# A hybrid encoder layer on one core: stores and small loads become steps of their own in the planner, VectorE and GpSimd are kept apart in its plan, and matmuls that depend on other engines are planned later

## The chip, the cores and the metric

The kernel runs on one core of one Trainium2 chip. A core has five engines with a queue of instructions each: TensorE (PE, with its weight loads shown apart as PEld), VectorE (DVE), ScalarE (ACT), GpSimd (POOL) and SyncE (SP), which here issues every DMA. Each engine works through its own queue in the order in which the program was written; semaphores hold an instruction until what it needs is there. The metric is the device time of one execution in microseconds.

## What is computed

One step of a one-layer streaming encoder, for 1024 frames of a new stream (the prompt) and 32 frames of a running one (the sample), in one array of 1056 frames. Cut to what matters:

```python
h = rmsnorm(x, g_mix_norm);  z = h @ w_in            # 1024 -> 8192
qa, ka, va, qr, kr, vr, g_ret, gate_a, gate_r = split(z)
qa, ka = rmsnorm(qa), rmsnorm(ka)                    # per head, 2 x 64
# 8 heads of differential attention, chunk-causal; sample: with a cache of 512 keys
s = einsum(qa, ka) * 64**-0.5;  p = softmax(s)       # two maps per head
o_a = rmsnorm((p[0] - lam * p[1]) @ va) * g_sub
# 8 heads of retention with decay, from a running state
o_r = rmsnorm((rotary(qr) @ rotary(kr).T * d_mat) @ vr + q @ S * q_decay) * silu(g_ret)
x = x + (sigmoid(gate_a) * o_a + sigmoid(gate_r) * o_r) @ w_o
x = x + (silu(h2 @ w_ff_gate) * (h2 @ w_ff_up)) @ w_ff_down      # h2 = rmsnorm(x), 2816 wide
y = x + sigmoid(rmsnorm(x) @ w_ple_gate) * (p_in @ w_ple)
# outputs: y, the new keys and values (ka, va), the final retention states
```

## The kernel before

Products in float32 accuracy are made of three float16 products: each operand is split in a high and a low part (`mm3`, lines L748 to L750 for the projection, L488 to L490 elsewhere).

The program has a head stage and then a merge and feed-forward stage. **The head stage** goes through 72 units, a unit being one head h (8) and one tile of frames i (9 tiles, the last with the 32 sample frames). For each unit PE makes two projections, A (q, k, v and rotary q, k) and, four units later (`LAG`), B (retention values and gates). Each is 8 times three matmuls of 128x512 into one of three PSUM banks `pj`.

What follows an A projection is `unit_a`: ACT takes the projection out of PSUM, DVE and GpSimd normalize and scale q and k, `kv` (L1055, GpSimd) is the key to be stored; SP stores it (L1056), transposes q and k by DMA (L1080 `q`, L1082 `kT`); PE makes the scores `sc` (L889 to L892), DVE the row maximum (L899), DVE or GpSimd the bias `nb` (L901), ACT the exponentials (L909); DVE combines the two maps and splits the result (L923 to L937; the high part by ACT L933 or DVE L935), SP transposes it by DMA (`aT`, L942), PE multiplies with v (`po`, L950 to L954), and the head's output `oa` is normalized (L971). `values` makes v and, on GpSimd, the rotation (L983 to L991).

What follows a B projection is `unit_b` with `retention`: PE transposes the rotated q and k (`pr`, L1144), DVE or ACT copies the result out (`copy`, L402: `qz` and `qT`), PE multiplies (L1157 to L1160), DVE masks (`inn`, L1163), PE multiplies again (`por`, L1165); then norm, gates and the sum with `oa` (L1230), a DMA transpose (`mixT`, L1244) and a store into scratch memory (`mix_d`, L1248). At the end the eight rows of `mix_d` are read back as `mixs`, the operand of the next stage. Beside this the weights of the next head are loaded, 1 MB at a time (L421), scaled and split (L473 to L481); `cache_steps` does so for the cached keys and values.

**What sets the order.** The order of PE, DVE, ACT and GpSimd, and with it that of the DMAs on SP, is made at build time by a planner, `Flow`. Each piece of work is a generator. It yields the engine that it needs and how long the planner shall take it to be (`V` for DVE, `S` for ACT, `G` for GpSimd, `M` for PE, `DM` and `X` for the DMA path, `either` where two engines will do), and then writes its instruction; `get` and `put` take and return buffers, `wait` and `set` are events, `delay` passes time. `Flow.run` takes the piece that can start first, by its own clock, and so fixes the program's order; a DMA that is written without a yield comes where its generator happens to be, right behind its producer. A result of DVE, ACT or GpSimd is taken to be usable after `LAT` = 0.13 more, and a matmul that comes behind such a step after another `MARGIN` = 0.3. On the chip none of these times is kept: only the order is.

The second stage (output projection, gate and up products in a seven-product scheme, and the first part of the down product) has a `Flow` of its own; the rest is written in program order.

Of the kernel before, what the change touches and what calls it, by code (L numbers as in the profile page):

```python
# [21 lines left out]
P = 128  # L22
# [24 lines left out]
MARGIN = 0.3  # L47
# [10 lines left out]

def V(n, f=1.0, x=0.0):
    return {"V": 0.07 + x + f * n / 960.0}  # L60
# [6 lines left out]
def G(n, x=0.0):  # L67
    return {"G": 0.15 + x + 0.0021 * n}
# [129 lines left out]
def kernel(  # L198
# [81 lines left out]
    def spread_max(amax, n, tag, at_bank=None):  # L280


        if at_bank is None:
            yield ("wait", "id")
        key, pool = at_bank or ("o", ps_o)
        yield ("get", key)
        yield M(0.1)
        pt = pool.tile([P, 512], F32, tag=key, name="mt")
        nc.tensor.transpose(out=pt[0:n, 0:P], in_=amax, identity=id32)
        yield V(P)  # L290
# [109 lines left out]

    def copy(e, out, in_):
        (nc.scalar.copy if e == "S" else ENG[e].tensor_copy)(out, in_)  # L402
# [3 lines left out]
    def load_block_steps(src, w, b, gi, tag, rowf, out, tail=False, due=None, late=None, hold=None):  # L406
# [19 lines left out]
        for q in range(4):  # L426
# [9 lines left out]
            yield V(512)  # L436
# [65 lines left out]
    with ExitStack() as pa:  # L502
# [98 lines left out]
        def const_b():  # L601
# [44 lines left out]
            yield V(128)  # L646
# [5 lines left out]
            yield V(128)  # L652
# [29 lines left out]
        def norm_x(i):  # L682
# [34 lines left out]
            for b in range(2):  # L717
# [12 lines left out]
                g = yield either(S(4 * R), V(4 * R))  # L730
                copy(g, hi, pt)
                yield V(4 * R)
# [29 lines left out]
        def fold(i, ps):  # L762
# [8 lines left out]
            yield V(P)  # L771
# [7 lines left out]
        def rms_small(ss, R, n, tag):  # L779

            yield G(0, 0.5 + 0.2 * n)
# [5 lines left out]
        def prep_head_a(h, w, e):  # L787
# [7 lines left out]
            s0 = s02[:, h % 2]  # L795
            nc.sync.dma_start(out=s0[0:64], in_=st0[h])
            gr = hp.tile([P, P], F32, tag="grn", name="grn", bufs=2)
            nc.sync.dma_start(out=gr, in_=grn[h])
# [8 lines left out]
        def cache_steps(h, dA, e):  # L807
# [24 lines left out]
            yield V(1, 1.0, 0.3)  # L832
# [45 lines left out]
        def attend(key, i, R, q4, sblocks, masked, vblocks, NK, sc_ap, do_ap):  # L878
# [3 lines left out]
            for ms in ((0, 1),) if NK <= 512 else ((0,), (1,)):  # L882
# [13 lines left out]
                yield V(NK * len(ms))  # L896
# [96 lines left out]
        def values(h, i, R, ps, kv, zr, dA, e, buf, key):  # L993
# [14 lines left out]
            yield V(P)  # L1008
# [9 lines left out]
        def unit_a(h, i, ps, dA, e):  # L1018
# [25 lines left out]
            yield V(256)  # L1044
# [11 lines left out]
            nc.sync.dma_start(out=kvo[h, t0:t0 + RT], in_=kv[0:RT])  # L1056
            yield ("later", ("kv", 3.0))
# [44 lines left out]
        def prep_head_b(h, w, e):  # L1102
# [8 lines left out]
            yield V(128)  # L1111
# [26 lines left out]
        def retention(h, i, R, vr, e, box):  # L1138
# [7 lines left out]
            g = yield either(V(128), S(128, -0.06))  # L1146
            copy(g, q0[0:64], pr[64:128, 0:P])
            g = yield either(V(128), S(128, -0.06))
# [12 lines left out]
            yield V(128)  # L1161
# [7 lines left out]
            yield V(128)  # L1169
# [11 lines left out]
            if i >= NT - 2:  # L1181
                nc.sync.dma_start(out=ro[i - (NT - 2), h], in_=Sq)

        def unit_b(h, i, ps, dB, e):
# [18 lines left out]
            yield V(P)  # L1203
# [14 lines left out]
            yield V(P, 1.0, 0.06)  # L1218
# [28 lines left out]
            yield X(0.05)  # L1247
            nc.sync.dma_start(out=mix_d[h, :, :, t0:t0 + RT], in_=mt[:, :, 0:RT])  # L1248
            yield ("later", ("mix", 2.2))
# [50 lines left out]
        def load_ple():  # L1300
# [4 lines left out]
            for n, (src, c, o) in enumerate(((pT, T, 0), (wple, D, 4 * T))):  # L1305
# [8 lines left out]
                for q, (k, cs) in enumerate(cuts):  # L1314
                    yield V(c // 2)
                    nc.vector.tensor_reduce(out=am4[:, q:q + 1], in_=st[:, k, cs], axis=AX.X, op=ALU.max, apply_absolute_value=True)
                yield V(4)
# [18 lines left out]
        def ple(part):  # L1336
# [3 lines left out]
            for m in (2 * part,):  # L1340
                for pair in (((m, 0), (m, 1)), ((m + 1, 0), (m + 1, 1)), ((m, 2), (m + 1, 2))):
                    for n, (j, c) in enumerate(pair):
# [8 lines left out]
                        g = yield either(S(CH), V(CH))  # L1351
# [14 lines left out]
        def last_mix():  # L1366
            for i in range(NT):
                yield ("wait", ("b", H - 1, i))
            nc.sync.dma_start(out=tail["mixs"][:, H - 1], in_=mix_d[H - 1])

        def stream():
# [10 lines left out]
            for s in range(NT * H + LAG):  # L1382
# [37 lines left out]
                if s >= LAG:  # L1420
# [16 lines left out]
            for part in range(4):  # L1437
# [3 lines left out]
                         ret=2, th=2, xc=3, su=1, ms=2))  # L1441
# [22 lines left out]
    with ExitStack() as pc:  # L1464
# [18 lines left out]
        with ExitStack() as pw:  # L1483
# [73 lines left out]
            def residual(c):  # L1557
# [10 lines left out]
                for m in range(KD):  # L1568
                    yield ("wait", ("wo", c, m))
                    yield V(CW, 1.0, 0.08)  # L1570
# [24 lines left out]
                yield V(4, 1.0, 0.1)  # L1595
                v = sm(4, "nbv")
                nc.vector.tensor_scalar(out=v[0:B], in0=ps[0:B, CW:CW + 4], scalar1=_f(1.0 / D), scalar2=EPS, op0=ALU.mult, op1=ALU.add)
                yield G(4, 0.2)
# [11 lines left out]
                for k in (0, 4, 1, 5, 2, 6, 3, 7):  # L1610
                    yield V(CW, 1.0, 0.08)
# [132 lines left out]
            def gu_sums(j, p):  # L1744
# [12 lines left out]
                def comb(out, in0, ps, op=ALU.add):  # L1757
                    yield V(CW, 1.0, 0.06)
# [331 lines left out]
```

## Time and profile before

| | us |
|---|---|
| median of three runs | 1901.42 (1895.13 to 1901.45) |
| the profiled execution | 1898.33 |
| its span, first to last instruction | 1896.5 |
| PE, DVE, ACT, GpSimd busy in the span | 1808.5, 1474.4, 1063.3, 715.1 |
| first matmul of a projection, last of a projection | 17.9, 1006.9 |
| first matmul of the output projection | 1038.9 |

A few words on how the profile is read. A line such as L950 is a line of the kernel before. "Busy" of PE counts a matmul until its modelled end; matmuls overlap, so that a 128x512 matmul is shown with some 0.38 us although the next one starts 0.216 us behind it. A loss on PE is therefore read best from one start to the next. A wait row names the engine, tile and line that waited, and behind the arrow what ended the wait; SPq is SyncE's queue, where a DMA that waits holds back all that is queued behind it. "Granted clock" is TensorE's clock as a share of the full one.

### The profile page before, as it was taken

What the parts mean: (1) busy time and instruction counts of PE and PEld (TensorE: products, weight loads), DVE (VectorE), ACT (ScalarE), POOL (GpSimd) and SP (SyncE); (2) the same over time, 40 slices, a digit from 0 to 9 for tenths busy, and PEclk for the clock granted to TensorE, in tenths of its full rate; (3) what the DMA queues carried; (4) which work ended last, traced back from release to release, by engine and by line L of the source; (5) the groups of instructions that cost most, each with busy time, mean ns of one, the idle gap of its engine ahead of it and who ended that gap; (6) DMA issues with size and microseconds to landing.
All of it is one profiled execution on the core that took longest, in us unless ns stands there. A gap on an engine that the chain in (4) does not pass through costs nothing.

```text
span 1896.5 us, 37208 instructions
## 1 busy us (share of the span) xinstructions
PE 1808.5 (95%) x13391; PEld 1152.9 (61%) x13391; DVE 1474.4 (78%) x3784; ACT 1063.3 (56%) x2762; POOL 715.1 (38%) x1161
## 2 busy tenths in 40 slices
PE   6889999999999989999998998999999999999999
PEld 3455455555555545555555686777777776666666
DVE  7878887887877878878886489999999986644364
ACT  7667766676675756767665345555555542101132
POOL 3646454454654554545441167323232300000010
PEclk9999999999999999999999999999999999999999
DMA  5344433444443433443438421221212116112031
GB/s 198 101 115 108 111 83 88 110 92 117 90 99 89 101 97 79 123 99 88 110 79 265 163 65 49 80 102 68 79 45 68 45 62 256 62 62 88 2 134 50
DMA packets 234251, 186.06 MB, mean 98 GB/s; under 512 B 187569, under 2 KB 214449, under 8 KB 226130
## 3 DMA queue, kind: packets, MB, share of 16 engines
q1 hardware_dynamic: 234066, 183.69, 35.0%
q8 instruction: 105, 1.72, 0.4%
q14 instruction: 80, 0.66, 0.1%
HBM read 113.09 MB, written 31.34 MB: 76 GB/s over the span
## 4 chain that ended last, share of the span: by engine, by line
PE 58%; DVE 17%; POOL 8%; ACT 7%; DMA 5%; issue 4%; SPq 0%; POOLq 0%; DVEq 0%; ACTq 0%
PE ps L488 9%; PE ps L490 9%; PE ps L489 9%; PE ps L1479 4%; PE pj L748 4%; PE pj L749 4%; PE ps L1478 4%; PE pj L750 4%; PE ps L1477 4%; DMA aT<-p 3%; ACT p L909 2%; DVE nm L899 2%; POOL qkr L784 2%; DVE w L481 1%; DVE w L1630 1%
## 5 line engine op out<-in xcount | busy, mean ns | idle before, releaser
L748 PE MATMUL pj<-w,xh 128*128 128x512 f16 x1024 | 390.8, 382 | 2.8 <-ACT w L479 2.8
L749 PE MATMUL pj<-w,xh 128*128 128x512 f16 x1024 | 390.6, 381 | 0.6 <-DVE w L481 0.6
L750 PE MATMUL pj<-w,xh 128*128 128x512 f16 x1024 | 390.4, 381 | 0.0
L489 PE MATMUL ps<-mixs,w 128*128 128x352 f16 (+1 forms) x960 | 262.5, 279 | 5.9 <-DVE mixs L1502 5.9
L488 PE MATMUL ps<-mixs,w 128*128 128x352 f16 (+1 forms) x960 | 262.4, 278 | 0.3 <-DVE o1c L244 0.3
L490 PE MATMUL ps<-mixs,w 128*128 128x352 f16 (+1 forms) x960 | 262.4, 278 | 0.0
L490 PEld LDWEIGHTS <-w 128*128 128x128 f16 x1736 | 170.9, 98 | 57.3 <-issue 6.0
L488 PEld LDWEIGHTS <-w 128*128 128x128 f16 x1736 | 171.1, 99 | 56.2 <-issue 4.8
L489 PEld LDWEIGHTS <-w 128*128 128x128 f16 x1736 | 170.8, 98 | 53.0 <-issue 3.6
L1635 POOL TENSOR_TENSOR st<-st 128x512 f32<-128x512 f32 x66 | 88.5, 1341 | 244.7 <-DVE w L1630 186.7
L750 PEld LDWEIGHTS <-xh 128*128 128x128 f16 x1024 | 100.5, 98 | 123.5 <-issue 3.8
L748 PEld LDWEIGHTS <-xh 128*128 128x128 f16 x1024 | 101.0, 99 | 91.6 <-issue 6.5
L909 ACT ACTIVATE p<-sc,nb,scs 128x896 f32<-128x896 f32 (+7 forms) x128 | 106.3, 831 | 87.6 <-POOL nb L901 52.5
L749 PEld LDWEIGHTS <-xh 128*128 128x128 f16 x1024 | 100.5, 98 | 87.3 <-issue 4.3
L488 PE MATMUL ps<-tT,w 128*128 128x352 f16 (+1 forms) x528 | 143.7, 277 | 0.0
L489 PE MATMUL ps<-tT,w 128*128 128x352 f16 (+1 forms) x528 | 143.6, 277 | 0.0
L490 PE MATMUL ps<-tT,w 128*128 128x352 f16 (+1 forms) x528 | 143.6, 277 | 0.0
L1630 DVE SCALAR_TENSOR_TENSOR w<-st,gus,w 128x512 f16<-128x512 f32 x132 | 140.6, 1066 | 0.1
L899 DVE TENSOR_REDUCE nm<-sc 128x1 f32<-128x640 f32 (+6 forms) x112 | 102.7, 917 | 26.1 <-PE sc L892 25.6
L1479 PE MATMUL ps<-a,w 128*128 128x352 f16 x312 | 97.5, 313 | 0.5 <-DVE w L1721 0.5
L1477 PE MATMUL ps<-a,w 128*128 128x352 f16 x312 | 97.5, 313 | 0.0
L1478 PE MATMUL ps<-a,w 128*128 128x352 f16 x312 | 97.5, 313 | 0.0
(422 smaller groups left out, 4650.4 us busy)
## 6 DMA issues: line engine op xcount, KB each, us to landing
st<-in_win_dram SPq DMA_DIRECT2D x30, 1024.0 KB, 5.3
st<-in_wgu_dram SPq DMA_DIRECT2D x22, 1024.0 KB, 4.8
st<-in_wdn_dram SPq DMA_DIRECT2D x16, 704.0 KB, 5.4
out_dram<-kv SPq DMA_DIRECT2D x64, 128.0 KB, 1.9
a_d<-a SPq DMA_DIRECT2D x9, 528.0 KB, 2.6
b<-a_d SPq DMA_DIRECT2D x9, 528.0 KB, 7.5
mixs<-mix_d SPq DMA_DIRECT2D x8, 528.0 KB, 6.5
pw_d<-pws SPq DMA_DIRECT2D x12, 352.0 KB, 4.2
```

The source lines that it names most:

```text
L488: nc.tensor.matmul(out=ps, lhsT=wh, rhs=ah, start=first, stop=False)
L489: nc.tensor.matmul(out=ps, lhsT=wh, rhs=al, start=False, stop=False)
L490: nc.tensor.matmul(out=ps, lhsT=wl, rhs=ah, start=False, stop=last)
L748: nc.tensor.matmul(out=ps, lhsT=xhi, rhs=w[:, k, 0], start=(k == 0), stop=False)
L749: nc.tensor.matmul(out=ps, lhsT=xhi, rhs=w[:, k, 1], start=False, stop=False)
L750: nc.tensor.matmul(out=ps, lhsT=xh[:, k, 1, t0:t0 + P], rhs=w[:, k, 0], start=False, stop=(k == KD - 1))
L899: nc.vector.tensor_reduce(out=nm[0:R, mc], in_=pv, axis=AX.X, op=ALU.max, negate=True)
L909: nc.scalar.activation(pt[0:R, 0:NK], ps[0:R, p0:p0 + NK], AF.Exp, bias=nb[0:R, m:m + 1], scale=sc_ap[0:R], accum_out=Z[0:R, m:m + 1])
L1477: nc.tensor.matmul(out=ps, lhsT=wt[:, 0, j], rhs=a[:, 0, cs], start=(first and j == js[0]), stop=False)
L1478: nc.tensor.matmul(out=ps, lhsT=wt[:, 1, j], rhs=a[:, 0, cs], start=False, stop=False)
L1479: nc.tensor.matmul(out=ps, lhsT=wt[:, 2, j], rhs=a[:, 1, cs], start=False, stop=(last and j == js[-1]))
L1630: nc.vector.scalar_tensor_tensor(out=w[:, i, 1], in0=src, scalar=s, in1=w[:, i, 0], op0=ALU.mult, op1=ALU.subtract)
```

## The change

Four things are changed; the arithmetic and the number of instructions stay (the choice of engine for the `either` steps aside).

1. `MARGIN` goes from 0.3 to 0.8: a matmul that depends on another engine is planned 0.5 later. This holds for both planners.
2. In the head stage's planner a step of DVE that is marked as working on SBUF (`V`, now an `Own`) and one of GpSimd (`G`) may not overlap. Steps that read or write PSUM, reductions and GpSimd's small power steps are marked `VP` and `GP`, which do not take the lock. Some forty yields are renamed so; two are shown.
3. Stores (`kvo`, `ro`, `mix_d`) become generators of their own, planned 2.0, 1.0 and 1.0 behind their producer, with 0.5 of the DMA path each.
4. Small loads (retention state, norm gains, cache) get a yield of the DMA path each, and the read-back of `mix_d` as `mixs` waits for the stores row by row.

```diff
-MARGIN = 0.3
+MARGIN = 0.8
...
+class Own(float):
+    pass
+
 def V(n, f=1.0, x=0.0):
+    return {"V": Own(0.07 + x + f * n / 960.0)}
+
+def VP(n, f=1.0, x=0.0):
     return {"V": 0.07 + x + f * n / 960.0}
...
 def G(n, x=0.0):
+    return {"G": Own(0.15 + x + 0.0021 * n)}
+
+def GP(n, x=0.0):
     return {"G": 0.15 + x + 0.0021 * n}
...
 class Flow:
-    def __init__(self, buffers):
+    def __init__(self, buffers, shared=False):
+        self.shared = shared
         self.free = {e: 0.0 for e in "MVSGD"}
+        self.port = {"V": 0.0, "G": 0.0}
...
                     start = max(c[3], self.free[e])
+                    if self.shared and isinstance(us, Own):
+                        start = max(start, self.port["G" if e == "V" else "V"])
...
             self.free[e] = start + us
+            if isinstance(us, Own):
+                self.port[e] = start + us
...
+    def store(out, in_, key, us, event=None):
+        yield ("delay", us)
+        yield X(0.5)
+        nc.sync.dma_start(out=out, in_=in_)
+        if event:
+            yield ("set", event)
+        if key:
+            yield ("delay", 2.5)
+            yield ("put", key)
...
-            nc.sync.dma_start(out=kvo[h, t0:t0 + RT], in_=kv[0:RT])
-            yield ("later", ("kv", 3.0))
+            flow.add(store(kvo[h, t0:t0 + RT], kv[0:RT], "kv", 2.0))
...
-            yield X(0.05)
-            nc.sync.dma_start(out=mix_d[h, :, :, t0:t0 + RT], in_=mt[:, :, 0:RT])
-            yield ("later", ("mix", 2.2))
+            flow.add(store(mix_d[h, :, :, t0:t0 + RT], mt[:, :, 0:RT], "mix", 1.0, ("m", h, i)))
...
-            nc.sync.dma_start(out=kc[0:64], in_=ckT[h])
-            nc.sync.dma_start(out=kc[64:128], in_=ckT[h])
-            nc.sync.dma_start(out=vc, in_=cv[h])
-            yield ("delay", 6.0)
+            for dst, src in ((kc[0:64], ckT[h]), (kc[64:128], ckT[h]), (vc, cv[h])):
+                yield X(0.9)
+                nc.sync.dma_start(out=dst, in_=src)
+            yield ("delay", 4.0)
...
-            yield V(NK * len(ms))
+            yield VP(NK * len(ms))
...
-            g = yield either(V(128), S(128, -0.06))
+            g = yield either(VP(128), S(128, -0.06))
...
         def last_mix():
-            for i in range(NT):
-                yield ("wait", ("b", H - 1, i))
-            nc.sync.dma_start(out=tail["mixs"][:, H - 1], in_=mix_d[H - 1])
+            for j in range(H):
+                for i in range(NT):
+                    yield ("wait", ("m", j, i))
+                yield X(0.5)
+                nc.sync.dma_start(out=tail["mixs"][:, j], in_=mix_d[j])
...
-                        for j in range(H - 1):
-                            nc.sync.dma_start(out=tail["mixs"][:, j], in_=mix_d[j])
...
-                         ret=2, th=2, xc=3, su=1, ms=2))
+                         ret=2, th=2, xc=3, su=1, ms=2), True)
```

What this does to the order is shown at two places. Line numbers after the change are some 30 higher (L1157 becomes L1187, L942 becomes L973, both stores become L423), the names stay.

The first is PE's queue in the retention of head 2, tile 6 (`pr` and `por` are its PSUM tiles, `pj` the projection that runs meanwhile), from the transpose to the next matmul of the same unit. Before:

```order
L1144 MATMUL pr<-cst_sb,qk 128x128
L748 LDWEIGHTS xh
L748 MATMUL pj<-w,xh 128x512
...
L750 LDWEIGHTS xh
L750 MATMUL pj<-w,xh 128x512
L1157 MATMUL pr<-qz_130,qT 128x128
L1159 MATMUL por<-S_134,qz_130 128x128
```

Six matmuls of the projection stand between L1144 and L1157. After the change the same place reads:

```order
L1174 MATMUL pr<-cst_sb,qk 128x128
L777 LDWEIGHTS xh
L777 MATMUL pj<-w,xh 128x512
...
L981 MATMUL po<-vcs,aT 128x128
...
L779 LDWEIGHTS xh
L779 MATMUL pj<-w,xh 128x512
L1187 MATMUL pr<-qz_130,qT 128x128
L1189 MATMUL por<-S_134,qz_130 128x128
```

Now nine matmuls of the projection and the fifteen short ones of another unit's `po` stand there.

The second is SP's queue at the `aT` transpose of head 3, tile 3 (`st` is a 1 MB load of weights, `mix_d` a store of the B side, `mixT` its transpose). Before:

```order
L1244 DMA_TRANSPOSE mixT<-ms 128x2x32
L1080 DMA_TRANSPOSE q_6735<-qst 128x2x128
L1082 DMA_TRANSPOSE kT<-qst 128x4x128
L421 DMA st<-in_win_dram 128x2048
L942 DMA_TRANSPOSE aT<-p 128x8x128
L1248 DMA mix_d<-mixT 256x1x32
```

The load stands ahead of the transpose, the store behind it. After:

```order
L1110 DMA_TRANSPOSE q_6682<-qst 128x2x128
L1112 DMA_TRANSPOSE kT<-qst 128x4x128
L1274 DMA_TRANSPOSE mixT<-ms 128x2x32
L423 DMA mix_d<-mixT 256x1x32
L973 DMA_TRANSPOSE aT<-p 128x8x128
L450 DMA st<-in_win_dram 128x2048
```

The load has moved behind the transpose and the store of `mix_d` ahead of it.

More of the change, by code (lines that the diff above doesn't have):

```diff
@@ L289, in spread_max @@
         nc.tensor.transpose(out=pt[0:n, 0:P], in_=amax, identity=id32)
-        yield V(P)
+        yield VP(P)
         mc = sm(1, tag + "mc")
@@ L435, in load_block_steps @@
                 continue
-            yield V(512)
+            yield VP(512)
             if rowf is None:
@@ L651, in const_b @@
             ls = sm(2, "ls")
-            yield V(128)
+            yield VP(128)
             nc.vector.tensor_reduce(out=ls, in_=lam_sb[:, 0].rearrange("p (b c) -> p b c", b=2), axis=AX.X, op=ALU.add)
@@ L729, in norm_x @@
                 hi, lo = [xh[:, ks, a, i * P:i * P + P] if i < NT - 1 else xs[:, ks, a * TS:(a + 1) * TS] for a in range(2)]
-                g = yield either(S(4 * R), V(4 * R))
+                g = yield either(S(4 * R), VP(4 * R))
                 copy(g, hi, pt)
-                yield V(4 * R)
+                yield VP(4 * R)
                 nc.vector.tensor_tensor(out=lo, in0=pt, in1=hi, op=ALU.subtract)
@@ L770, in fold @@
             nc.scalar.copy(su, psv[:, :, 1])
-            yield V(P)
+            yield VP(P)
             nc.vector.tensor_tensor(out=suz[:, :, 0:TS], in0=psv[:, :, 0], in1=su, op=ALU.add)
@@ L779, in rms_small @@
         def rms_small(ss, R, n, tag):
-            yield G(0, 0.5 + 0.2 * n)
+            yield GP(0, 0.5 + 0.2 * n)
             r = sm(n, tag + "r", 6)
@@ L795, in prep_head_a @@
             s0 = s02[:, h % 2]
+            yield X(0.5)
             nc.sync.dma_start(out=s0[0:64], in_=st0[h])
             gr = hp.tile([P, P], F32, tag="grn", name="grn", bufs=2)
+            yield X(0.5)
             nc.sync.dma_start(out=gr, in_=grn[h])
@@ L831, in cache_steps @@
             ar = sm(2, "car")
-            yield V(1, 1.0, 0.3)
+            yield VP(1, 1.0, 0.3)
             nc.vector.tensor_tensor(out=ar[:, 0:1], in0=pt[:, 0:1], in1=kbound, op=ALU.max)
@@ L1007, in values @@
                                      scale=e["ddec"][0:R, b:b + 1])
-            yield V(P)
+            yield VP(P)
             nc.vector.scalar_tensor_tensor(out=vh[0:R, i, 1], in0=ps[0:R, 256:384], scalar=vs_, in1=vh[0:R, i, 0],
@@ L1043, in unit_a @@
             nc.scalar.activation(sq[0:R], zg[0:R], AF.Square, scale=0.125)
-            yield V(256)
+            yield VP(256)
             ss = sm(4, "qss", 6)
@@ L1110, in prep_head_b @@
             dB = w[1]
-            yield V(128)
+            yield VP(128)
             nc.vector.tensor_reduce(out=mbr, in_=e["gr"], axis=AX.X, op=ALU.max, apply_absolute_value=True)
@@ L1160, in retention @@
             nc.tensor.matmul(out=pr[:, 384:512], lhsT=qk[:, (h * NT + i) % NQ], rhs=vr, start=True, stop=True)
-            yield V(128)
+            yield VP(128)
             inn = wk.tile([P, P], F32, tag="inn", name="inn")
@@ L1168, in retention @@
             gT = _f((1.0 - 2.0 ** (-5 - h)) ** (P if i < NT - 1 else TS))
-            yield V(128)
+            yield VP(128)
             Sn = S2[:, (h * NT + i) % 2]
@@ L1181, in retention @@
             if i >= NT - 2:
-                nc.sync.dma_start(out=ro[i - (NT - 2), h], in_=Sq)
+                flow.add(store(ro[i - (NT - 2), h], Sq, None, 1.0))
         def unit_b(h, i, ps, dB, e):
@@ L1201, in unit_b @@
                                  scale=hdB[0:R, 1:2])
-            yield V(P)
+            yield VP(P)
             gu = wk.tile([P, P], F32, tag="gu", name="gu")
@@ L1217, in unit_b @@
             r = yield from rms_small(ss, R, 1, "or")
-            yield V(P, 1.0, 0.06)
+            yield VP(P, 1.0, 0.06)
             of = wk.tile([P, P], F32, tag="orf", name="orf", bufs=3)
@@ L1314, in load_ple @@
                 for q, (k, cs) in enumerate(cuts):
-                    yield V(c // 2)
+                    yield VP(c // 2)
                     nc.vector.tensor_reduce(out=am4[:, q:q + 1], in_=st[:, k, cs], axis=AX.X, op=ALU.max, apply_absolute_value=True)
-                yield V(4)
+                yield VP(4)
                 am = sm(1, "wam", 3)
@@ L1350, in ple @@
                             yield ("get", "p")
-                        g = yield either(S(CH), V(CH))
+                        g = yield either(S(CH), VP(CH))
                         if n == 0:
@@ L1594, in residual @@
                                          rhs=ones32[:, 0:1], start=(j == 0), stop=(j + 1 == n))
-                yield V(4, 1.0, 0.1)
+                yield VP(4, 1.0, 0.1)
                 v = sm(4, "nbv")
                 nc.vector.tensor_scalar(out=v[0:B], in0=ps[0:B, CW:CW + 4], scalar1=_f(1.0 / D), scalar2=EPS, op0=ALU.mult, op1=ALU.add)
-                yield G(4, 0.2)
+                yield GP(4, 0.2)
                 r = sm(4, "nbr")
@@ L1610, in residual @@
                 for k in (0, 4, 1, 5, 2, 6, 3, 7):
-                    yield V(CW, 1.0, 0.08)
+                    yield VP(CW, 1.0, 0.08)
                     nc.vector.scalar_tensor_tensor(out=xf[:, k], in0=xf[:, k], scalar=gS[:, 1, k:k + 1], in1=ps[:, 0:CW],
@@ L1757, in comb @@
                 def comb(out, in0, ps, op=ALU.add):
-                    yield V(CW, 1.0, 0.06)
+                    yield VP(CW, 1.0, 0.06)
                     nc.vector.tensor_tensor(out=out, in0=in0, in1=ps, op=op)
```

7 lines of the change are left out of this document (4 added, 3 removed).

## The prediction

> **What bounds the kernel now.** I read the busy time by stage first, then PE's waits in the longest stage, then the timeline at single waits, and last SP's queue. The stages (columns: window, its length, busy time of PE, PEld, DVE, ACT and GpSimd with instruction counts, granted clock, DMA share, GB/s):
>
> ```profile
> 0.00:50.00 50.00, 35.53 (x154) 18.18 (x155) 37.67 (x120) 36.84 (x79) 19.64 (x39) 1.00 0.60 200
> 50.00:1005.00 955.00, 902.99 (x6283) 505.00 (x6281) 766.42 (x2263) 655.84 (x1942) 500.01 (x957) 0.99 0.42 98
> 1005.00:1040.00 35.00, 29.37 (x208) 19.43 (x205) 22.10 (x75) 18.55 (x45) 2.96 (x7) 0.92 0.93 312
> 1040.00:1180.00 140.00, 128.88 (x1070) 95.86 (x1068) 105.99 (x200) 60.20 (x127) 69.05 (x60) 0.95 0.28 93
> 1180.00:1897.00 717.00, 711.74 (x5689) 514.47 (x5686) 542.26 (x1131) 291.88 (x573) 123.44 (x101) 1.00 0.23 81
> ```
>
> PE is busy almost throughout, so its work is the floor and only its waits can be won: 5 us behind 1180, where nothing is to be had, and 955 - 903 = 52 us in the head stage, which is the part that the change reorders. Who ends them there (total, times, longest):
>
> ```profile
> PE po L950 <- DMA aT<-p: 23.9, 16, 4.5
> PE pr L1157 <- DVE qT L402: 5.1, 9, 1.0
> PE sc L889 <- ACT p L909: 5.1, 8, 1.3
> PE pr L1157 <- ACT qT L402: 4.3, 7, 1.1
> PE t L722 <- DVE w L712: 3.5, 2, 1.9
> PE sc L889 <- DMA kT<-qst: 3.1, 3, 1.3
> PE por L1165 <- DVE inn L1163: 3.1, 6, 0.9
> PE mt L314 <- DVE wamh L447: 2.3, 4, 0.7
> ```
>
> These 50 us are nearly all of it, and no projection (L748) is among them: PE never waits for a `pj` bank. But idle time hides a part, as one place shows (start, duration):
>
> ```profile
> 405.28 0.28 PE L1144 MATMUL pr<-cst_sb,qk 128*128 128x128 f32 x1
> 405.39 0.38 PE L748 MATMUL pj<-w,xh 128*128 128x512 f16 x1
> ...
> 406.26 0.38 PE L749 MATMUL pj<-w,xh 128*128 128x512 f16 x1
> 406.47 0.38 PE L750 MATMUL pj<-w,xh 128*128 128x512 f16 x1
> 406.94 0.49 PE L1157 MATMUL pr<-qz,qT 128*128 128x128 f32 x2
> ```
>
> A matmul of 512 columns takes 0.216 from start to start; L1157 starts 0.47 behind L750, so 0.25 us is lost although no gap is shown. Counted so, start to start against the usual spacing of each form over the 6283 matmuls of the window, the loss is 71 us: some 27 at L950, 14 at L1157, 12 at L889, 7 at L1165, 4 at L722, 3 at L314, 4 elsewhere. That is the purse. A part of the clock comes on top (below).
>
> **The change part by part.** *MARGIN.* Six projection matmuls, 1.3 us, stand between L1144 and L1157 at this place, and the chain through two copies took 0.25 longer. Over all 72 units the order before has 1.8 us of PE work there, the order after 2.6; between L1160 and L1165 it is 1.6 and 2.0 (row counts of the two orders, each row at the spacing of its form in the trace). The same 0.8 taken off each of the 72 losses at L1157 leaves 2 of 14; 0.4 at L1165 leaves 2.5 of 7. **Minus 12 and minus 4.5.** The work that fills the gap is the projection that has to be done anyway. What is late next is the rest of the unit, the norm and the gates, whose result is first wanted after the unit's own `oa`, and that is early.
>
> *Scores.* L889 waits for the one `sc` bank, until ACT's exponentials end, and for `kT`. The 0.5 of MARGIN taken off its losses leaves 5 of 12, but transposes of q now stand right behind a 1 MB load 14 times where it was 7. What such a neighbour does, from issue to landing for L1080 (min, median, max) and in one wait at `aT`:
>
> ```profile
> DMA to landing us min/median/max: 2.3/2.8/6.3
> ...
> 448.69 0.53 SPq L421 DMA_DIRECT2D st<-in_win_dram  x1
> 449.32 1.24 SPq L942 DMA_TRANSPOSE aT<-p  x1
> ...
> 455.40 0.23 PE L950 MATMUL po<-vh,aT 128*128 128x128 f16 x1 [0.74 <-DMA aT<-p]
> ```
>
> At the worst 7 x 3.5 = 24 us come back; at the best nothing, since the distance from the end of an A projection to its scores grows from 16 to 20 us of PE work. I take 3 back, near the lower end, because 3.8 us of new distance exceeds the 3.5: **minus 4** for L889 with that.
>
> *The `aT` transposes, stores and loads.* Two causes show. One is the load just seen: the transpose took 6 us to land. In the order after, `aT` stands right behind a load 5 times, not 15. The other is a store that waits on SP:
>
> ```profile
> 530.79 0.36 SPq L421 DMA_DIRECT2D st<-in_win_dram  x1
> 538.87 0.33 SPq L1056 DMA_DIRECT2D out_dram<-kv  x1
> 539.31 1.20 SPq L942 DMA_TRANSPOSE aT<-p  x1
> ...
> 536.25 0.48 DVE L937 SCALAR_TENSOR_TENSOR p<-p,lsc 128x256 f16<-128x256 f32 x1
> ...
> 541.78 0.23 PE L950 MATMUL po<-vh,aT 128*128 128x128 f16 x1 [1.06 <-DMA aT<-p]
> ...
> SPq L1056 <- POOL kv L1055: 118.2, 42, 8.9
> SPq L1248 <- DMA mixT<-ms: 55.3, 42, 3.8
> ```
>
> The data of the transpose were ready at 536.7; SP stood at the store of `kv` until 538.9, and PE lost 1.2 us. The last two rows are all such waits of the stores in the stage. In the plan a store now comes 1 to 2 us later, so more of what is ready passes it. Against this, `aT` stands right behind a store of `mix_d` 40 times, not 22, and a store waits 55.3 / 42 = 1.3 us for its transpose. From the scores to `po` there is 0.8 us more PE work than before (13.0 against 12.2), but half of that was there already as lost time. Bounds: all 27 go, or, with 18 x 1.3 = 23 us of new SP waits and no cover, as good as none do. I take 12 left, **minus 15**: by their neighbours in SP's rows, 13 of the 19 large losses have one of the two causes right ahead of them.
>
> *The lock in the plan.* 65 instructions leave GpSimd for DVE, and 16 splits go from DVE to ACT (count, min/median/max ns):
>
> ```profile
> L901 POOL TENSOR_SCALAR nb<-nm,scs x68: 282/358/1576, 54.7 to 982.8; 128x1 f32<-128x1 f32 x44, 128x2 f32<-128x2 f32 x24
> L901 DVE TENSOR_SCALAR nb<-nm,scs x28: 195/208/279, 89.7 to 973.4; 128x1 f32<-128x1 f32 x20, 128x2 f32<-128x2 f32 x8
> L1052 DVE TENSOR_TENSOR z<-z,gqk x49: 407/424/673, 38.2 to 974.1; 128x256 f32<-128x256 f32 x49
> L1234 DVE TENSOR_TENSOR mx<-mx,orf x44: 270/292/559, 85.9 to 1013.4; 128x128 f32<-128x128 f32 x44
> L1234 POOL TENSOR_TENSOR mx<-mx,orf x28: 447/456/1482, 107.1 to 1023.0; 128x128 f32<-128x128 f32 x28
> L935 DVE TENSOR_SCALAR p<-p,lsc x30: 273/542/1039, 60.9 to 995.5; 128x640 f16<-128x640 f32 x9, 128x384 f16<-128x384 f32 x5, 128x896 f16<-128x896 f32 x5, 128x512 f16<-128x512 f32 x4
> L933 ACT ACTIVATE p<-p,lsc x42: 388/828/1148, 67.4 to 986.7; 128x256 f16<-128x256 f32 x8, 128x640 f16<-128x640 f32 x7, 128x768 f16<-128x768 f32 x7, 128x1024 f16<-128x1024 f32 x5
> ```
>
> DVE gets 32 `nb` at 0.208, 19 operations on `z` at 0.424, 14 of 128x128 and 5 copies at 0.292: 20 us, less 16 splits at 0.542, 9: plus 12 us on 766. ACT gets the 16 at 0.828, 13 us; GpSimd loses over 20. All three have 200 to 450 us of idle time in the stage, so this costs PE nothing by itself; were DVE's cover gone, 12 us. Medians of the DVE rows lie 4 to 8% above their minima, so that keeping the two engines apart can give DVE 0.04 x 766 = 30 us at most, beside PE's work; I take 0 (as a rival: below).
>
> *Clock.* Two waits and the windows of 50 us around them:
>
> ```profile
> 302.07 0.29 PE L950 MATMUL po<-vh,aT 128*128 128x128 f16 x1 [2.33 <-DMA aT<-p]
> ...
> 300.00:350.00 50.00, 46.15 (x305) 25.64 (x306) 34.85 (x103) 31.20 (x96) 22.52 (x48) 0.93 0.41 93
> 650.00:700.00 50.00, 44.38 (x301) 24.22 (x300) 37.24 (x124) 29.48 (x95) 26.68 (x51) 0.93 0.41 106
> ```
>
> 0.93 of 50 us is 3.5 us lost, behind a wait of 2.3 us in the one and of 4.5 (the longest at L950) in the other; a third window, 100 to 150, loses about 1.5. Of these 8.5 us between none and all go with the waits; **minus 5**. [...]
>
> *The rest.* L722 and L314 minus 1. The read-back of `mixs` and the last loads are ordered anew between 1005 and 1040, where the DMAs are busy 0.93 of the time: between 3 us won and 3 lost, I take 0. Stage two changes only in where the few matmuls behind L314 and L1608 stand: 0, from 2 us won to 2 lost, as PE has 5 us of waits in 717.
>
> Sum: -12 -4.5 -4 -15 -5 -1 = -41.5; new waits that a faster PE meets, as every chain then has less time, I put at a tenth, +4. **-37 us** on the profiled execution's 1898.3 (span 1896.5 and 1.8 around it): **1861 us**. The median, 1901.4, is 3 us above that execution; I leave this in the range.
>
> **The rivals.** *Stores still in the way:* SP waits at `mix_d` ahead of `aT` as reckoned; the 15 us stay away and the clock's 5 with them. 1881 us, chance 0.16. For it: 40 against 22. Against it: the plan puts such an `aT` a microsecond or more behind the landing.
>
> *The waits only move:* the units' pace is set by DVE, 766 us busy and 12 more, and what PE no longer loses at one line it loses at the next. 1892 to 1901 us, about the same as before; 0.10. Against it: DVE is idle for a fifth of the stage.
>
> *Slower, by the `pj` banks:* ACT takes the projections out of three banks and now has 16 more splits of `p`, each of which must wait for DVE, with the drains queued behind. If ACT falls back by two projections, 2 x 24 x 0.216 = 10.4 us, PE waits at L748; 0.35 us at each of the 144 projections is 50 us, and the sum becomes +13, 1911 us. Below 10.4 us of delay it costs nothing. 0.06: today not one wait at L748 is for a bank.
>
> [...]
>
> *It does not do what it says* (on the chip only the order is kept, so the two engines still meet) changes nothing in the sum, which takes nothing from the lock.
>
> **How the numbers follow.** Forecast, from 1845 to 1878: 0.60. The rivals, in order: 0.16, 0.10, 0.06, 0.08. Faster by over 0.5% (10 us, about what a measurement of this kernel can tell from no change) holds for the forecast, the first and the last: 0.84. The same: 0.10; slower: 0.06. The range reaches from the large gain to the edge of no change, 1836 to 1900, and leaves out some 0.06 above and 0.05 below.
>
> **What would show it.** In the profile after: PE's waits at L1187 (before L1157) under 3 us in total, at L1195 under 2, at L981 (before L950) about 10 with none over 3; no window of the head stage with a clock under 0.97; the output projection's first matmul near 1003, 36 us earlier; SP's waits at the stores shorter. I am wrong if L981 keeps its 24, if waits at L777 for a bank appear, or if the stage's end stays where it is while the named waits fall.

## The result and the profile after

| | before | after |
|---|---|---|
| median, us | 1898.79 (1895.13 to 1901.45, 4 runs) | 1849.46 (1848.95 to 1850.32, 4 runs) |
| ratio, 95% interval | | 0.9742 (0.972 to 0.9764) |
| span of the profiled execution | 1896.5 | 1847.9 |
| last matmul of a projection (start) | 1006.9 | 960.5 |
| first matmul of the output projection | 1038.9 | 993.2 |
| PE, DVE, ACT, GpSimd busy | 1808.5, 1474.4, 1063.3, 715.1 | 1790.0, 1460.0, 1071.7, 674.5 |

The forecast was 1861 in 1836 to 1900, so the time lies inside the range, 12 us below the forecast. The busy times by stage of the kernel after, in the columns of before:

```profile
0.00:50.00 50.00, 37.33 (x165) 18.68 (x166) 38.81 (x119) 37.30 (x79) 19.59 (x37) 1.00 0.62 202
50.00:960.50 910.50, 888.46 (x6306) 508.01 (x6303) 752.38 (x2328) 665.56 (x1956) 466.76 (x895) 1.00 0.45 105
960.50:995.00 34.50, 28.71 (x185) 18.18 (x182) 22.80 (x74) 21.08 (x50) 2.11 (x5) 0.95 0.89 286
995.00:1135.00 140.00, 127.08 (x1103) 97.29 (x1101) 105.82 (x196) 59.14 (x124) 71.28 (x62) 0.96 0.28 95
1135.00:1848.00 713.00, 708.46 (x5648) 511.49 (x5645) 540.15 (x1124) 288.63 (x567) 114.75 (x100) 1.00 0.23 81
```

The span is 48.6 us shorter, and the head stage 46.4 (1006.9 to 960.5): the change did its work where it was expected, in PE's idle time, which fell there from 52 us to 910.5 - 888.5 = 22. PE's waits in this stage (total, times, longest):

```profile
PE po L981 <- DMA aT<-p: 10.8, 10, 4.6
PE sc L920 <- ACT p L940: 2.8, 2, 2.0
PE pr L1187 <- ACT qT L431: 2.3, 2, 1.5
PE pr L1174 <- DVE o0c L262: 1.8, 1, 1.8
...
PE pj L777 <- DVE B1p L266: 1.2, 1, 1.2
PE sc L920 <- DMA kT<-qst: 0.9, 1, 0.9
PE sc L920 <- DMA q<-qst: 0.6, 1, 0.6
```

L981 is L950 of before, L1187 is L1157, L1195 is L1165, L920 is L889, L777 is L748. `po` has 10.8 us where it had 23.9, L1187 has 2.5 (with a row of 0.2 that is not shown) where L1157 had 9.4, and L1195 is gone from the list. SP's waits in the stage:

```profile
SPq L423 <- POOL kv L1086: 93.4, 34, 8.1
SPq L423 <- DMA mixT<-ms: 61.3, 49, 4.0
```

The store of `kv` holds SP up for 93 us instead of 118, that of `mix_d` for 61 instead of 55.

Read so far, the prediction looks confirmed line by line. The experiments ask whether the three parts of the change did this, each its own share.

### The profile page after: what moved, and what is told of

It is laid out like the page before. It is cut to its first block, busy times and chain, and to the rows that moved or that the text cites. A ratio compares the mean times of both kernels' runs of the same rounds, so it can differ in the third digit from the quotient of the medians.

```text
span 1847.9 us, 37184 instructions
## 1 busy us (share of the span) xinstructions
PE 1790.0 (97%) x13391; PEld 1153.7 (62%) x13391; DVE 1460.0 (79%) x3838; ACT 1071.7 (58%) x2773; POOL 674.5 (37%) x1096
## 4 chain that ended last, share of the span: by engine, by line
PE 82%; DVE 8%; DMA 4%; ACT 2%; POOL 2%; issue 2%; SPq 0%; ACTq 0%; POOLq 0%; DVEq 0%
PE ps L517 10%; PE ps L518 10%; PE ps L519 10%; PE pj L777 10%; PE pj L778 9%; PE pj L779 9%; PE ps L1507 4%; PE ps L1505 4%; PE ps L1506 4%; DMA aT<-p 2%; PE sc L920 2%; PE sc L923 2%; PE pj L788 1%; PE po L981 1%; PE po L985 1%
## 5 line engine op out<-in xcount | busy, mean ns | idle before, releaser
L777 PE MATMUL pj<-w,xh 128*128 128x512 f16 x1024 | 390.0, 381 | 3.1 <-ACT w L508 1.7
L777 PEld LDWEIGHTS <-xh 128*128 128x128 f16 x1024 | 101.0, 99 | 89.6 <-issue 2.1
L940 ACT ACTIVATE p<-sc,nb,scs 128x256 f32<-128x256 f32 (+7 forms) x128 | 106.1, 830 | 51.8 <-DVE nb L932 40.8
```

The lines of the kernel that those rows point to most:

```text
L777: nc.tensor.matmul(out=ps, lhsT=xhi, rhs=w[:, k, 0], start=(k == 0), stop=False)
L940: nc.scalar.activation(pt[0:R, 0:NK], ps[0:R, p0:p0 + NK], AF.Exp, bias=nb[0:R, m:m + 1], scale=sc_ap[0:R], accum_out=Z[0:R, m:m + 1])
```

## The experiments

All loss figures below are sums of mine over the trace, in us: for each matmul of the head stage, from 50 us to the last 128x512 matmul of a projection (1002.7 in before, 954.4 in after), the time from the start before it to its own, less the usual spacing of its form (the method of the prediction). The half-clock column is what matmuls lost in stretches with a granted clock of 0.5. Names of lines are those of before. `L1157+` is L1157 and L1165 together; up to the last matmul of any projection it is 24 in before and 6 in after. Each ratio compares with runs of before in the same round; their medians are 1896.5 to 1898.8.

| kernel | MARGIN | lock | stores | us | ratio, 95% interval | L950 | L1157+ | L889 | other | half clock |
|---|---|---|---|---|---|---|---|---|---|---|
| before | 0.3 | no | no | 1898.79 | 1 | 27.2 | 23.5 | 11.8 | 8.7 | 5.6 |
| m_only | 0.8 | no | no | 1869.76 | 0.9859 (0.9838 to 0.9881) | 13.5 | 10.8 | 9.5 | 8.8 | 1.5 |
| l_only | 0.3 | yes | no | 1879.28 | 0.9912 (0.989 to 0.9934) | 17.7 | 13.4 | 4.9 | 12.8 | 6.5 |
| s_only | 0.3 | no | yes | 1886.09 | 0.9943 (0.9925 to 0.9962) | 10.5 | 26.2 | 13.4 | 9.3 | 3.0 |
| no_lock | 0.8 | no | yes | 1884.87 | 0.994 (0.9918 to 0.9963) | 17.0 | 28.0 | 10.0 | 7.9 | 4.3 |
| no_m | 0.3 | yes | yes | 1865.74 | 0.9826 (0.9805 to 0.9847) | 18.0 | 4.3 | 7.0 | 8.9 | 3.5 |
| no_s | 0.8 | yes | no | 1864.48 | 0.983 (0.981 to 0.985) | 7.6 | 5.9 | 11.2 | 19.7 | 7.8 |
| after | 0.8 | yes | yes | 1849.46 | 0.9742 (0.972 to 0.9764) | 12.5 | 3.7 | 5.3 | 6.6 | 2.0 |
| after_m75 | 0.75 | yes | yes | 1880.01 | 0.9907 (0.9884 to 0.993) | 24.7 | 3.6 | 6.5 | 16.8 | 11.9 |
| no_lock_m75 | 0.75 | no | yes | 1894.15 | 0.9982 (0.997 to 0.9994) | 9.8 | 20.8 | 19.7 | 13.6 | 12.4 |
| slow_v | 0.8 | no | yes | 1906.84 | 1.0052 (1.0037 to 1.0067) | 21.3 | 4.2 | 15.2 | 19.5 | 12.8 |
| nb_v | 0.8 | no | yes | 1865.76 | 0.9845 (0.9818 to 0.9871) | 16.8 | 11.3 | 4.4 | 9.8 | 3.3 |
| nb_g | 0.8 | yes | yes | 1878.46 | 0.9901 (0.9884 to 0.9919) | 19.3 | 4.2 | 4.8 | 20.3 | 12.2 |
| lock_nb_v | 0.8 | yes | yes | 1872.64 | 0.9868 (0.9852 to 0.9885) | 13.8 | 6.4 | 6.1 | 16.7 | 8.3 |

The stretch from the last projection to the output projection is not in the table. It takes 28 to 41 us (32 in before, 33 in after), and took back 7 to 8 us of what `m_only` and `s_only` won in the head stage.

### One part alone

`m_only` is before with

```diff
-MARGIN = 0.3
+MARGIN = 0.8
```

> The kernel before with MARGIN at 0.8 and nothing else. Theory (the terms of the forecast, which add up): the losses at PE's L1157 and L1165 fall to what the full change shows (about 5 and 1 us, start to start, from 17 and 7), those at L722 and L314 to 1 each, L889 loses 2 to 3 of its 12, and L950 keeps its 24 us of waits, because the DMA transposes stand where they stood: 16 to 24 us faster than before, 1875 to 1883. Rival, the parts need each other: what PE no longer loses at these lines it loses at L950 (waits of 35 us or more there) and the time is within 8 us of before. Rival, MARGIN is nearly all of it: L950 falls to about 12 as well, and the time is under 1865.

It gave 27 us, more than the theory's 16 to 24, and its reason is not the theory's: L1157+ fell to 10.8, not to the 6 expected, but L950, which was to keep its 24, fell by half, nearly to the 12 of the last rival, though no DMA's yield was touched.

`l_only` is before with `V`, `G`, `VP`, `GP` of after and the lock:

```diff
-                         ret=2, th=2, xc=3, su=1, ms=2))
+                         ret=2, th=2, xc=3, su=1, ms=2), True)
```

> The kernel before with the lock in the plan and nothing else (VectorE and GpSimd kept apart, MARGIN 0.3, stores and loads as before). Theory: no gain from the lock, within 6 us of before, 1893 to 1905; PE's waits at the two lines of pr and por stay. Rival, the lock works by what it does to the plan: every chain through both engines is planned longer, the scores stand 19.6 us of PE work behind their projection where it was 16, and the waits at the scores and at po fall by half: 1875 to 1885. Rival, the lock works on the chip: VectorE's and GpSimd's instructions of the head stage get shorter (VectorE 767 us busy to 750 or less at the same work), with a like gain. Rival, it costs: 12 us more of VectorE's work show as waits, 1910.

17 us faster: my 0 for the lock was wrong, and the time is that of the rival by the plan, 1875 to 1885. The lines are not quite its: the scores' loss more than halved, but L1157+ fell by 10 as well, at an unchanged MARGIN. DVE's busy time in the stage fell from 768 to 754 us, with 41 more instructions; that is close to the sign of the rival on the chip, and is taken up below.

`s_only` is before with the `store` generators, the loads' yields and the read-back of the change, `MARGIN = 0.3`, no lock.

> The kernel before with stores and small loads as steps of their own and nothing else (no lock, MARGIN 0.3). Theory: the waits at po (L950 of before) fall from 24 to about 12 us and the clock's 5 us come back: 12 to 20 us faster, 1879 to 1887; SP's waits at the kv store fall from 118 to under 100. Rival, stores are not the cause: a transpose of p still stands right behind a 1 MB load 14 times, as before, and po keeps 20 us or more: within 6 us of before.

It gave 10 us, just short of the theory's 12 to 20. L950 did what was expected of it (27.2 to 10.5), but SP's waits at the `kv` store stayed at 113 us, not under 100; L1157+ and the scores grew by 4 together.

### The change without one part

`no_lock` is after with

```diff
-                         ret=2, th=2, xc=3, su=1, ms=2), True)
+                         ret=2, th=2, xc=3, su=1, ms=2))
```

> The kernel after without the lock in its plan (MARGIN 0.8, stores and loads as steps). Theory: the lock is worth nothing, so within 5 us of the kernel after, 1845 to 1855. Rival, the lock lengthens the plan's distances: transposes of p stand right behind a 1 MB load 16 times, not 5, and the scores 17.0 us behind their projection, not 19.9, so the waits at po are 20 us or more where they are 11, and the time is 1862 to 1875.

The time is 1885: 35 us lost, beyond even the rival's range, and not at the rival's place, as `po` waits 14.6 us and not 20. MARGIN with stores is 15 us slower than MARGIN alone, so the parts do not add. And at `MARGIN` 0.8, L1157+ has 28 us, more than before. `no_m` is the reverse, after with `MARGIN = 0.3`:

> The kernel after with MARGIN at 0.3 (lock, stores and loads stay). Theory of the forecast: the terms at pr, por, part of the scores and the small lines come back, 20 us: 1866 to 1874. Rival: the lock gives the distances that MARGIN gives, so little is lost, 1850 to 1857. Rival: MARGIN is most of it, 1875 to 1882, where the lock alone stands (1879).

The time is just under what the forecast expected. Its reason is refuted: here L1157+ has only 4.3 us. The order puts 2.4 us of PE work between L1144 and L1157 in `no_lock` (the median unit) and 1.8 in `no_m`, as in before. These are PE's waits ahead of the line in `no_lock`:

```profile
PE pr L1187 <- ACT qT L431: 9.3, 9, 3.4
PE pr L1187 <- DVE qT L431: 1.7, 3, 1.2
PE pr L1187 <- DVE cac L262: 0.9, 1, 0.9
```

In the same list of `no_m` the line does not appear; counted from start to start, L1157 loses 17.7 us in `no_lock` and 2.2 in `no_m`. So with more work ahead of it the matmul waits, with less it does not. What differs is the other side of the wait. The second copy ends 1.73 us behind the transpose on average in `no_lock`, 1.35 in before, and 1.09 in `no_m` (1.24 in after), because ACT and DVE arrive late or in time at the first one: it starts 0.96 us behind the transpose in `no_lock`, 0.27 in `no_m`. Ahead of six of the nine losses over 0.6 us in `no_lock`, the engine of a copy had just waited for a result of GpSimd (`z`, `mx`, `nb` or a power step).

`no_s` is after with the DMA code of before, the read-back of `mixs` too:

```diff
-            flow.add(store(kvo[h, t0:t0 + RT], kv[0:RT], "kv", 2.0))
+            nc.sync.dma_start(out=kvo[h, t0:t0 + RT], in_=kv[0:RT])
+            yield ("later", ("kv", 3.0))
...
-            for dst, src in ((kc[0:64], ckT[h]), (kc[64:128], ckT[h]), (vc, cv[h])):
-                yield X(0.9)
-                nc.sync.dma_start(out=dst, in_=src)
-            yield ("delay", 4.0)
+            nc.sync.dma_start(out=kc[0:64], in_=ckT[h])
+            nc.sync.dma_start(out=kc[64:128], in_=ckT[h])
+            nc.sync.dma_start(out=vc, in_=cv[h])
+            yield ("delay", 6.0)
```

> The kernel after with stores, small loads and the read-back as before (lock and MARGIN 0.8 stay). Theory of the forecast: without them the 15 us at po and the clock's 5 come back: 1865 to 1872. Rival, from the runs so far (MARGIN with stores was 11 us faster than before where MARGIN alone was 27): the stores are worth nothing, 1845 to 1855.

1864.5 is at the forecast's edge, again for another reason. PE's waits at `po`, with the stores as before, are the smallest of all kernels:

```profile
PE po L979 <- DMA aT<-p: 3.7, 6, 1.6
PE po L979 <- DVE z L1079: 1.9, 1, 1.9
```

The 15 us that stay away were lost at L748 (9.6), the scores and the clock.

### What the lock does

On the chip the two engines are not kept apart: between 50 and 960 us, GpSimd is busy for 466 us of after, and in 389 of them DVE is busy too; in `no_lock` it is 398 of 490. (The 467 of 478 and 474 of 503 in the expectation below count time twice where an engine's own instructions overlap in the trace.) These are 83 and 81%, the share for which DVE is busy in this window anyway. So the lock acts through the order. Two ideas of how were tried. One was that DVE's steps are planned too short, and the lock makes them longer:

```diff
-    return {"V": Own(0.07 + x + f * n / 960.0)}
+    return {"V": Own(0.15 + x + f * n / 960.0)}
```

and the same in `VP`, without the lock (`slow_v`).

> The kernel after without the lock, but every VectorE step planned 0.08 us longer (0.07 becomes 0.15 in V and VP). Theory, from the four runs so far: the lock is worth some 35 us beside MARGIN and the stores, not because the engines are apart on the chip (VectorE and GpSimd overlap for 467 of GpSimd's 478 us in the stage with it, 474 of 503 without), but because it makes the plan's VectorE later, whose steps are planned too short (128 elements: 0.203 planned, 0.284 and more in the trace). Then the longer step does the same without a lock: 1845 to 1860. Rival, the lock itself: keeping the two engines apart is what matters, and this kernel stays where the one without the lock is, 1878 to 1892. Rival, luck of the plan: any time from 1850 to 1890.

It is the slowest of all, outside the ranges of the theory and of both rivals. L1157+ did fall to 4.2, so planned slack for DVE mends that place without a lock; but the plan now gave more to GpSimd (766 us busy in the span, 713 in `no_lock`), and the excess went to the scores, to L314 and L950, and to the clock. The cost holds for the second planner too, where some 9 us were lost that belong to no question here.

The other idea came from ACT's waits for GpSimd between 50 and 950 us; the first rows are of before, then after, then `no_lock`:

```profile
ACT p L909 <- POOL nb L901: 58.8, 50, 3.4
ACT ms L1238 <- POOL mx L1234: 12.8, 13, 2.2
```

```profile
ACT p L940 <- POOL nb L932: 10.2, 14, 1.3
ACT ms L1268 <- POOL mx L1264: 2.5, 5, 1.5
```

```profile
ACT p L940 <- POOL nb L932: 69.4, 59, 3.6
ACT ms L1268 <- POOL mx L1264: 18.9, 19, 1.7
```

The exponentials wait for the bias `nb`, a 128x1 operation, and behind them in ACT's queue stand the copies of `pr` and the drains of the projections. With the lock the plan gives 32 more of the 96 to DVE. The row for those left on GpSimd in after, against DVE's:

```profile
L932 DVE TENSOR_SCALAR nb<-nm,scs x60: 196/205/501, 54.9 to 936.0; 128x1 f32<-128x1 f32 x41, 128x2 f32<-128x2 f32 x19
L932 POOL TENSOR_SCALAR nb<-nm,scs x36: 312/613/1192, 77.2 to 918.0; 128x1 f32<-128x1 f32 x23, 128x2 f32<-128x2 f32 x13
```

`nb_v` is `no_lock` with all `nb` on DVE; `lock_nb_v` is after with the same edit; `nb_g` is after with `nb` always on GpSimd:

```diff
-                g = yield either(V(1, 1.0, 0.06), G(1, 0.2))
+                g = yield V(1, 1.0, 0.06)
```

> The kernel after without the lock, with the bias nb always on VectorE (before it was either engine's, by the plan). Theory: what the lock changed is which engine makes nb. ACT waits for nb from GpSimd 59 to 69 us in the stage without the lock and 10 to 14 with it, and behind the exponential that waits stand the copies of pr and the drains of pj; so this kernel has ACT's waits for GpSimd under 30 us, PE's losses at L1187 and L1195 under 6 us (23 without the lock), and the time is 1850 to 1865, most of the way from 1885 to the 1849 with the lock. Rival, the lock works by other means (distances of the scores, order of the rotation): 1878 to 1892, though ACT's waits for nb go.

> The kernel after, lock and all, with nb always on GpSimd. Theory: ACT's waits for nb come back (50 us or more in the stage) and with them most of what the lock brought: 1870 to 1890. Rival, the lock works by other means: 1846 to 1858.

> The kernel after, lock and all, with nb always on VectorE. Theory: some of the 10 us that ACT still waits for nb goes, but PE loses only 3 us at the scores behind ACT: 1840 to 1852. Rival: VectorE, 40 more instructions of 0.2 us, becomes late for PE: 1855 to 1865.

`nb_v` won 19 us over `no_lock`, to 1865.8, a hair above the range: ACT's waits for GpSimd fell from 93 us to 11 and the scores from 10.0 to 4.4, L1157+ from 28.0 to 11.3, not under 6. `nb_g` lost 29 against after and has its waits back:

```profile
ACT p L940 <- POOL nb L932: 57.7, 55, 3.7
```

Yet it lost nothing at L1157+ (4.2) or the scores (4.8); its excess is at L950, L314, L748 and in the clock. And `lock_nb_v`, which was to stay or gain, lost 23, more than its rival had it. Neither result can be read as the price of `nb`, before it is known what a new plan is worth by itself.

### A new plan of the same kind

Both kernels with `MARGIN = 0.75` differ from after and from `no_lock` by 0.05 us in that one number.

> The kernel after without the lock, with MARGIN 0.75 in place of 0.8: a change too small to mean anything, which deals another plan. Theory: the loss without the lock is a matter of the plan's times, not of one plan, so it stays within 8 us of the run with 0.8: 1877 to 1893. Rival, luck of the plan: the time moves by more than 8 us, towards the 1870 of MARGIN alone or beyond, and then differences of this size between single plans tell little.

> The kernel after with MARGIN 0.75 in place of 0.8, a change that means nothing in itself and deals another plan of the same kind. Theory, from the eleven runs so far: a plan of this kind is worth 1860 to 1872, as with the other changes to it (1864, 1866, 1873, 1878), and the kernel after is a good draw among them: 1855 to 1872, with PE's losses at L1187 and L1195 still small (under 7 us, as in every plan with the lock and one other part) and the excess at po, the scores, the head weights and the projections' banks. Rival, the three parts add up to what the kernel after shows: 1845 to 1854.

Without the lock the time moves by 9 us, just beyond the theory's 8 and away from the 1870 of the rival; with it by **31 us**: 1849.5 becomes 1880.0, further off than even the expectation had it. L1157+ stayed small there, as expected (3.6). The stage and the waits of `after_m75`:

```profile
50.00:988.00 938.00, 897.85 (x6230) 509.54 (x6229) 753.20 (x2329) 660.52 (x1944) 455.96 (x886) 0.98 0.44 101
```

```profile
PE po L981 <- DMA aT<-p: 21.4, 14, 3.2
PE mt L332 <- DVE wamh L476: 8.1, 6, 3.0
PE sc L920 <- ACT p L940: 3.3, 3, 2.7
PE pj L777 <- DVE gu L1235: 3.0, 4, 0.9
```

Here L950 has nearly as much as in before, with the new stores in place. One of its waits, and the rows that lead to it:

```profile
892.29 0.47 DVE L968 SCALAR_TENSOR_TENSOR p<-p,lsc 128x256 f16<-128x256 f32 x1
894.30 0.35 SPq L423 DMA_DIRECT2D out_dram<-kv  x1
894.76 0.36 SPq L1338 DMA_DIRECT2D st<-in_wple_dram  x1
895.21 1.22 SPq L973 DMA_TRANSPOSE aT<-p  x1
...
900.58 0.29 PE L981 MATMUL po<-vh,aT 128*128 128x128 f16 x1 [3.19 <-DMA aT<-p]
```

`p` is ready at 892.8; SP reaches the transpose at 895.2, behind the `kv` store and a load, and it lands some 5 us later. Both causes named in the prediction still exist with the change. By the DMA right ahead of the transposes, the larger losses at L950 (over 0.5 us) come behind a load 7 times in before (17 us), twice in after (6), 4 times in `after_m75` (9.5, and 3 more times behind a `kv` store, another 4). Where they fall is what the plan deals. By its own clock `Flow` charges a 1 MB load 2.9 us of the DMA path; on the chip, where only the order is kept, SP issues the transpose of these rows 0.45 us behind the load.

## Why the prediction was right, and where it was not

**The bound: right.** The purse was PE's loss in the head stage; 71 and 6 of clock became 28 and 2, 47 us less, and the stage is 46 us shorter.

**MARGIN, -16.5 at L1157 and L1165: the size is right (23.5 became 3.7), the step failed.** It took the chain behind L1144 as fixed and the distance as what counts. `no_lock` and `no_m` show that the chain's end moves more than the distance does: the copies stand in line behind what ACT and DVE wait for. MARGIN alone took 13 of the 23, but with stores and no lock none; lock and stores without it took 19. At these lines the plans agree: the six with the lock and another part have 3.6 to 6.4, those without the lock 10.8 to 28.0, `slow_v` aside.

**The lock, 0: wrong.** I set it to 0 because the medians of the rows lie near their minima, so that keeping the engines apart could save little on the chip. GpSimd's rows of two operations of the prediction's list (L1234 and L1052 there) read after the change:

```profile
L1264 POOL TENSOR_TENSOR mx<-mx,orf x17: 452/455/763, 172.1 to 956.6; 128x128 f32<-128x128 f32 x17
L1083 POOL TENSOR_TENSOR z<-z,gqk x10: 720/724/1702, 57.5 to 929.0; 128x256 f32<-128x256 f32 x10
```

The median, 0.455, is what it was (0.456), but a median does not show the tail. These are the 1702 and another of the long ones, each with the DVE instruction beside it:

```profile
57.28 1.34 DVE L741 SCALAR_TENSOR_TENSOR w<-w,xrg 128x1024 f32<-128x1024 f32 x1
57.50 1.70 POOL L1083 TENSOR_TENSOR z<-z,gqk 128x256 f32<-128x256 f32 x1
...
436.11 0.41 DVE L1081 TENSOR_TENSOR z<-z,qkr 128x256 f32<-128x256 f32 x1
436.26 0.57 POOL L1264 TENSOR_TENSOR mx<-mx,orf 128x128 f32<-128x128 f32 x1 [0.23 <-DVE mx L1260]
```

GpSimd started while DVE worked on two inputs from SBUF, and ended 0.58 and 0.31 us behind DVE's end; the medians of the same operations are 0.72 and 0.455, 0.14 more in both, as if all but 0.14 us of the work had stood until DVE was done. This is no exception: in the head stage of before, 371 operations of GpSimd start with more than 0.14 us of such a DVE instruction still to go, and 341 of them last longer by just what was left beyond the 0.14, to within 0.03 us. Behind DVE's reductions, which also run beside GpSimd, the median excess is 0.002 us (113 operations). The forecast took nothing for this and was wrong there: of the 28 operations at L1234 in before, 13 were held up so.

What the lock in the plan saves there is still not much. Against the short end of each form (its tenth percentile over all runs), GpSimd loses 85 us in this way in before and 82 in after. DVE, where it starts behind GpSimd, loses 43 and 26; the 30 us that I called the most that could be had was no bound. For DVE the plans agree: 24 to 31 us in the seven with the lock, 35 to 44 in the seven without. How much of this reached PE, no run here separates. What I missed besides is that a lock in a planner is also a change of who does what and of how much room each step has. I counted the 65 moved instructions as load (12 us for DVE) and not as waits taken out of ACT's queue (72 us of waits for GpSimd became 13).

**Stores and loads, -15 at L950: the size came (27.2 to 12.5), the cause is not shown.** `no_s` has 7.6 with the old stores, `after_m75` 24.7 with the new ones; the four kernels with the old DMA code have 27.2, 13.5, 17.7 and 7.6, the ten with the new one 9.8 to 24.7. The two causes at SP are real, as the place above shows, but what the change does to their number can't be told from what a new plan deals.

**Scores, -4:** 11.8 became 5.3, -6.5. **Clock, -5:** the granted clock gave away 8.5 us of the stage before and 3.4 after, -5.1; of these, matmuls lost 5.6 and 2.0. The wait of 2.3 us that the prediction names for one of these losses had another of 0.9 us 3.3 us ahead of it, and one of 2.2 us in before (at 599.1) and one of 2.4 us in `after_m75` (at 542.7) have no half clock at them. So which single wait suffices is not shown. **L722 and L314, -1:** -5.6, in this plan. **New waits, +4:** 3.9, at L777 and L1174 (2.0 and 1.9 by the same sums, 0.4 of it in before). **Stage two and the read-back, 0:** 857.6 became 854.7 from the output projection's start, and 32 from there back to the last projection became 33.

Of the signs named beforehand, L1187, L1195, the 10 us at L981 and the `kv` store came; the longest wait at L981 is 4.6, not under 3, and one window has a clock under 0.97:

```profile
50.00:100.00 50.00, 43.80 (x237) 22.48 (x235) 41.45 (x124) 36.91 (x107) 29.07 (x51) 0.93 0.39 100
```

A wait at L777 for a bank, one of the signs of being wrong, appears with 0.2 us (`gu`); the 1.2 in the list above is for weights (`B1p`).

**What the number rests on.** Four pairs of the eight combinations differ in one part alone: the mean over them is -20 us for the lock (-5 to -35), -15 for MARGIN (-1 to -27), -6 for the stores (+15 to -15). With a neighbouring plan 31 or 9 us away, no single pair settles anything: the stores' mean can't be told from nothing, and of the lock's and MARGIN's the sign is likely and the size is not known. Whether the lock's share comes by `nb`, by the room it leaves for DVE, by what DVE no longer loses to GpSimd or by several of these stays open: `nb_v` speaks for the first, L1157+ of `slow_v` and `nb_g` for the second. Every changed plan but `slow_v` was faster than before (`no_lock_m75` by 3 us only), which would fit a poor draw in before as well; and after is the best of the 13. The six plans with the lock and at least one other part lie between 1849 and 1880, with a mean of 1868. That the measured time was so near the forecast is therefore in part luck, and the steps above say which part was reasoned.

**The rivals.** *Stores still in the way* is what `after_m75` shows: 24.7 at L950 and 11.9 of clock, 1880, the price I had set at 1881. *The `pj` banks* are real, though not by ACT's delay: PE's waits at L748 for DVE's steps on the bank (`vh`, `gu`) are none in before, 0.2 us in after, and 8.2 and 7.9 in `no_s` and `lock_nb_v`, a sixth of the 50 I had reckoned. The fourth chance, 0.08, was for a gain larger than forecast, from keeping DVE and GpSimd apart. The direction is right, by 12 us, and the two engines do hold each other up in the trace; but the order took only 17 of DVE's 43 us and 4 of GpSimd's 85 from that. *It does not do what it says* holds on the chip in the main, and, against what I wrote, that did not make the lock worth nothing.

## What to carry to other kernels

Where a planner with a greedy choice fixes the order, change a number that means nothing (here 0.05 us of a margin) and time it, before a difference is put down to a part of the change; search such numbers at the end, as this one is worth 31 us. A wait at a matmul has two sides: look at when the producer's engine got to its step and what it stood behind (here a 128x1 operation on GpSimd ahead of ACT's exponential), not only at the distance on PE. A term that comes out at its size is not a mechanism shown; undo the part and look at the same line. And a median near the minimum does not show that nothing is held up: look at what ran beside the long ones.

## What was not expected of the hardware

In `after_m75` more was lost than PE's waits: these cost 52 us of the stage and the half clock another 12, where after has 28 and 2. No wait of that stage is longer than 3.2 us, and the clock falls to 0.5 six times. One window, and the stretch at half clock in it:

```profile
50.00:100.00 50.00, 36.98 (x194) 19.49 (x193) 42.12 (x122) 33.85 (x98) 25.64 (x46) 0.81 0.52 131
64.30:81.40 17.10, 9.15 (x40) 5.28 (x41) 13.49 (x51) 13.13 (x41) 9.17 (x18) 0.50 0.30 69
```

The half clock sets in at 64.3, behind two waits of 0.9 and 1.0 us and in one of 1.1, all between 60.8 and 65.1 us, and waits of 2.7 and 2.1 us fall into it. At 0.81 of the clock these 50 us lose up to 9.5 us in one place. The other thing was that DVE and GpSimd, planned apart, overlap as before (for 389 of GpSimd's 466 us between 50 and 960, where before has 396 of 481), and that they still hold each other up, by the sums above for 82 us of GpSimd's time and 26 of DVE's.
